# Sample attention scores: one float32 product per key block in place of three split ones

## The chip, the cores and the metric

The kernel runs on one core of a Trainium2 chip. The metric is the device time of one execution in microseconds (us). Engines are named as in the profile: PE is TensorE's matmul row and PEld its weight loads, DVE is VectorE, ACT is ScalarE, POOL is GpSimd, SP is the engine that issues most DMAs.

## The reference, cut to what matters

One layer of a hybrid decoder handles a prompt of 1024 tokens and eight samples of eight new tokens each. Every sample has 1024 cached positions, in pages that a table names. Two attention groups of six heads read them: stick-breaking attention and forgetting attention (FoX). For both, the scores of the new tokens against the cached keys are

```python
kb_all = jnp.concatenate([gather_pages(cache_sb_k[l], page_table), kb], axis=1)
b_out = stick_breaking(qb, kb_all, vb_all, q_pos, k_pos)
kc_all = jnp.concatenate([gather_pages(cache_fox_k[l], page_table), kc], axis=1)
c_out = forgetting_attention(qc, kc_all, vc_all, F[:, past:], F, q_pos, k_pos)
# in both: z = einsum('bthd,blhd->bhtl', q.astype(float32), k.astype(float32)) * HEAD_DIM ** -0.5
```

Everything is float32, and the change concerns only these products `z` over cached keys.

## The kernel before, in words

Nearly all matmuls of this kernel work on values that are split by hand: a float32 value x becomes a high part (x rounded to the type float32r) and a low part (x minus the high part, again float32r), and a product of two values is the sum of high by high, high by low and low by high: three matmuls into the same PSUM bank. ACT usually makes the high part by a copy that rounds, and DVE the low part by a subtraction.

The program runs in stages: the input projections; then the prompt's attention (`prompt_attention`) beside the last projections; then, from about 402 us, `sample_attention` beside the rest of the prompt's attention; then the rest of `sample_attention` beside `merge` (the output projection, tile `prod`); then, from about 846 us, the feed-forward network. Where two generators run side by side, `conduct` takes turns between them by weights written into their `yield`s; after that a scheduler arranges the instructions of each engine's queue. Each engine works through its queue in order.

`sample_attention` goes through 32 steps t (group FoX first, then stick-breaking; in each group four pairs of samples; in each pair two halves of the pages for each of the two samples). In a step:

- `k_load` fetches 512 cached key rows by an indirect DMA on POOL (tile `kr`, three buffers).
- `k_tr` runs three times (p = 0, 1, 2, a pair of heads each). PE transposes four blocks of 128x128 into a PSUM bank (tile `str`, L713). ACT rounds the bank into the high part of `kt` (L717), DVE subtracts to get the low part (L718).
- `qk` of the step before does the scores: for each p three matmuls of 512 columns (tile `sqk`, L748), with the queries' high or low part as the stationary operand. `queries` picks them out of `qz`, which `build_q` fills for each pair of samples (L674).
- After a pair's two halves the scores go to the softmax (FoX, DVE L756) or the sigmoids (stick-breaking, ACT L760 and L761). `a_tr` transposes the pair's weights (tile `satr`, L802) and splits them (tile `ats`, L804 and L805); `v_split` splits value rows (tile `vh`, L816 and L817), and `value` multiplies (tile `spv`, L829).

The prompt's attention uses `aqk` (scores), `atr` (transposes of the weights, split by ACT L576 and DVE L577) and `apv` (values).

PSUM's eight banks are two rings: three banks for the uses marked "a", five for those marked "b" (`NBANK`, `BANKS`). A use takes the next bank of its ring when the one that stood there has been read out. `sqk`, `satr`, `spv`, `apv` and `prod` are in the ring of three; `str`, `atr`, `aqk`, `spick`, `stat` and `spread` in the ring of five.

Of the kernel before, what the change touches and what calls it, by code (L numbers as in the profile page):

```python
# [10 lines left out]
F32 = mybir.dt.float32  # L11
F32R = mybir.dt.float32r
I32 = mybir.dt.int32
AF = mybir.ActivationFunctionType
OP = mybir.AluOpType
# [28 lines left out]
RING = {"at": 5, "at_s": 2, "at_g": 2, "vh": 4, "kt": 3, "kr": 3, "vr": 3, "sa_x": 3, "vo": 2, "zn": 2, "hl": 2,  # L44
        "k32": 2, "ko": 2, "vt": 1, "wraw": 2, "wsplit": 5, "pvt": 2, "sl": 2}
# [5 lines left out]


NBANK = {"a": 3, "b": 5}
BANKS = {"pqk": "a", "ptok": "a", "kout": "a", "apv": "a", "sqk": "a", "satr": "a", "spv": "a", "prod": "a",
         "fgu": "a", "fgs": "b", "spread": "b", "fgt": "b", "aqk": "b", "atr": "b", "str": "b", "spick": "b", "gate": "b",
         "stat": "b", "fout": "b"}

# [42 lines left out]
def tile_decode_step(ctx, tc, x_prompt, x_sample, cache_sb_k, cache_sb_v, cache_fox_k, cache_fox_v,  # L100
# [5 lines left out]
    V, A, G, T, S = nc.vector, nc.scalar, nc.gpsimd, nc.tensor, nc.sync  # L106

    def f(ap):
        return ap.bitcast(F32)

    def pool(stack, name, bufs=1, space=None, side=None):
        kw = {} if space is None else {"space": space}
        if space is not DRAM:
            kw["reuse_waits"] = "tile"
        return stack.enter_context(tc.tile_pool(name=name, bufs=bufs, side=side, **kw))
# [58 lines left out]
    kn, vn, qn = {}, {}, {}  # L174
# [8 lines left out]
    def bank(shape, use):  # L183
        return ps.tile(shape, F32, name=use, tag=BANKS[use], bufs=NBANK[BANKS[use]])

# [457 lines left out]
    def sample_attention(sa):  # L643

        cks_, cvs_ = (cache_sb_k, cache_fox_k), (cache_sb_v, cache_fox_v)
        sos, kts, scs, gts, ats, vhs, krs, vrs, pzs, pvs, mns, dts = ({} for _ in range(12))
        def where_k(t):

            return 1 - t // 16, t // 4 % 4, t % 2, t // 2 % 2
# [8 lines left out]
        c2 = sa.tile([128, C_END - C_NSB], F32, name="c2")  # L658
        S.dma_start(c2, consts[:, C_NSB:C_END])

        qz = sa.tile([128, 1216], F32R, name="qz")
        V.memset(f(qz), 0.0)
        zns = {}

        def build_q(u):

            g, sp = 1 - u // 4, u % 4
            qv = qz[:, 0:1200].rearrange("p (x c) -> p x c", c=400)
            for e in range(2):
                er = slice(e * 64, e * 64 + 64)  # L670
                for si in range(2):
                    src = f(qn[g][er, :, :, (2 * sp + si) * 8:(2 * sp + si) * 8 + 8])
                    o = si * 128 + e * 8
                    V.tensor_copy(qv[er, :, o:o + 200].rearrange("p x (a c) -> p x a c", c=8)[:, :, 0:25:24], src)  # L674

        def queries(p, a, si):
            o = p * 384 + a * 192 + si * 64
            return qz[:, o:o + 128]

        def new_scores(g):  # L680
# [27 lines left out]
        def k_tr(t, p):  # L708
            if p == 0:
                kts[t] = []  # L710
            pt = bank([128, 4, 128], "str")
            for j in range(4):
                T.transpose(pt[:, j, :], krs[t][:, j, p * 128:p * 128 + 128], ident)  # L713
            kt = sa.tile([128, 2, 512], F32R, name="kt", bufs=RING["kt"])
            kts[t].append(kt)
            ptf = pt.rearrange("p j k -> p (j k)")
            A.copy(kt[:, 0], ptf)  # L717
            V.tensor_tensor(kt[:, 1], ptf, f(kt[:, 0]), op=OP.subtract)  # L718

        def by_row(x):  # L720
            return x[:, 0:SP_].rearrange("q (p r) -> q r p", r=8)
# [18 lines left out]
        def qk(t):  # L740
            g, sp, si, hf = where_k(t)
            u = t // 4
            if si == 0:
                pzs[t // 2] = bank([128, 512], "sqk")
            pz = pzs[t // 2]
            for p in range(3):
                for n_, (a, b) in enumerate(((0, 0), (0, 1), (1, 0))):
                    T.matmul(pz, lhsT=queries(p, a, si), rhs=kts[t][p][:, b], start=si == 0 and p == 0 and n_ == 0,  # L748
                             stop=si == 1 and p == 2 and n_ == 2)
            del kts[t], krs[t]  # L750
            if si:
                pz = pzs.pop(t // 2).rearrange("q (r p) -> q r p", p=128)
                sc = by_row(scs[u])[:, hf * 4:hf * 4 + 4]
                if g:
                    mn = mns[u]
                    V.tensor_tensor_reduce(sc, pz, by_row(dts[u])[:, hf * 4:hf * 4 + 4], 1.0,  # L756
                                           mn[:, 0:1] if hf else 3.0e38, op0=OP.add, op1=OP.min,
                                           accum_out=mn[:, hf:hf + 1])
                else:
                    A.activation(sc, pz, AF.Sigmoid, scale=-1.0)  # L760
                    A.activation(by_row(gts[u])[:, hf * 4:hf * 4 + 4], pz, AF.Sigmoid)  # L761
# [99 lines left out]
        NT_ = 32  # L861
        mks = {}
        build_q(0)
        for t in range(NT_ + SVL + 2):
            tv = t - SVL
# [12 lines left out]
            if t < NT_:  # L878
                for p in range(2):
                    k_tr(t, p)  # L880
                    yield 0.43
            if 0 <= t - 1 < NT_:
                qk(t - 1)
                if t < NT_ and t % 4 == 0:
                    build_q(t // 4)
                yield 1.95
            if t < NT_:
                k_tr(t, 2)
                yield 0.43
# [327 lines left out]
    sa = pool(psa, "sa")  # L1217
    ppc = ExitStack()
    pcs.append(pool(ppc, "pc", side="right"))
    sam = sample_attention(sa)  # L1220
    conduct([(att, P_W3A[0]), (sam, P_W3A[1])], True)
    ppc.close()
# [395 lines left out]
    for f0, nf in [(0, 1)] + [(x, FCH) for x in range(1, NFF, FCH)]:  # L1618
# [8 lines left out]
        for i in (8, 0, 1, 2, 3, 4, 5, 6, 7):  # L1627
            o = slice(i * 128, i * 128 + 128)
# [42 lines left out]
```

## Time and profile before

| | us |
|---|---|
| median of 3 runs | 1602.29 (1601.11 to 1602.63) |
| the profiled execution's own time | 1605.99 |
| its span in the trace | 1604.1 |

The profiled execution took 3.7 us more than the median, and 1.9 us of it lie outside the span. The page gives the busy time of each engine, 40 slices of the span with the granted TensorE clock, the DMA queues, the chain of work that ended last, and groups of instructions. "idle before" in a group is time in which the engine had nothing to do just before these instructions, with the engine and line whose end released it.

### The profile page before, as it was taken

The page shows a single profiled execution, that of the slowest core. Times are in us where ns is not written, and L with a number is a line of the kernel's source. Part 1 is how long each engine was busy: PE and PEld are TensorE (multiplying, and loading weights), DVE is VectorE, ACT ScalarE, POOL GpSimd, SP SyncE. Part 2 cuts the span into 40 slices and gives each one's busy share as a digit, 9 for nine tenths or more (in the row PEclk, how much of TensorE's full clock was granted, in tenths as well). Part 3 has the DMA queues.
Part 4 walks back from the last instruction along what each step waited for, and adds up shares of the span by engine and source line. Part 5 has one row for each costly group of instructions (what it writes and reads, how often), then busy time and mean ns, then how long its engine had stood idle before and what let it go on. Part 6 is the DMA issues. An engine that isn't in the chain of part 4 may idle for free.

```text
span 1604.1 us, 26359 instructions
## 1 busy us (share of the span) xinstructions
PE 1509.9 (94%) x9580; PEld 1394.2 (87%) x9580; DVE 1033.4 (64%) x1887; ACT 703.9 (44%) x1472; POOL 679.9 (42%) x775
## 2 busy tenths in 40 slices
PE   7999999888799989988997999999999999999997
PEld 6999998888688878877887999999999997888886
DVE  5432368866698988988769565555555557555554
ACT  6424257455477788864434233333333323111113
POOL 1203375546535655565315544444454435111112
PEclk9999999999799999989998999999999999999999
DMA  6155565355869775675433122222222218322202
GB/s 179 50 168 172 192 198 162 92 156 164 263 181 264 218 207 167 212 266 160 129 144 87 55 71 75 74 71 82 75 75 81 82 60 330 109 82 81 82 1 112
DMA packets 148741, 217.60 MB, mean 136 GB/s; under 512 B 19156, under 2 KB 111684, under 8 KB 148612
## 3 DMA queue, kind: packets, MB, share of 16 engines
q1 hardware_dynamic: 138868, 163.72, 32.7%
q0 software_dynamic: 9744, 52.20, 9.9%
q8 instruction: 76, 1.25, 0.3%
q14 instruction: 53, 0.43, 0.1%
HBM read 163.95 MB, written 51.92 MB: 135 GB/s over the span
## 4 chain that ended last, share of the span: by engine, by line
PE 47%; DVE 4%; DMA 2%; POOL 1%; issue 1%; ACT 0%; SPq 0%; DVEq 0%; POOLq 0%; ACTq 0%
PE fout L1635 5%; PE fout L1634 5%; PE fgs L1362 5%; PE fgs L1360 5%; PE fgs L1361 5%; PE fout L1637 5%; PE fgu L1360 4%; PE fgu L1362 4%; PE fgu L1361 4%; PE prod L1152 1%; DMA lr<-linv 1%; PE prod L1153 1%; PE prod L1155 1%; PE fgu L1435 1%; PE fgu L1434 1%
## 5 line engine op out<-in xcount | busy, mean ns | idle before, releaser
L1634 PE MATMUL fout<-foh,g_h 128*128 128x512 f32 x378 | 148.1, 392 | 0.9 <-POOL g_h L1584 0.9
L1635 PE MATMUL fout<-fol,g_h 128*128 128x512 f32 x378 | 148.1, 392 | 0.6 <-DVE fol L1580 0.6
L1638 DVE TENSOR_TENSOR z<-fout,z 128x512 f32<-128x512 f32 x128 | 86.7, 688 | 95.1 <-PE fout L1637 95.0
L817 POOL TENSOR_TENSOR vh<-vr,vh 128x384 fp32r<-128x384 f32 x96 | 102.7, 1088 | 74.0 <-ACT vh L816 55.5
L1360 PE MATMUL fgu<-xh,ws 128*128 128x272 f32 x456 | 131.8, 289 | 0.0
L1360 PE MATMUL fgs<-th,ws 128*128 128x272 f32 x456 | 131.7, 289 | 0.0
L1362 PE MATMUL fgs<-th,ws 128*128 128x272 f32 x456 | 131.6, 289 | 0.0
L1362 PE MATMUL fgu<-xh,ws 128*128 128x272 f32 x456 | 131.5, 288 | 0.0
L1361 PE MATMUL fgu<-xl,ws 128*128 128x272 f32 x456 | 131.1, 287 | 0.0
L1361 PE MATMUL fgs<-tl,ws 128*128 128x272 f32 x456 | 131.0, 287 | 0.0
L1637 PE MATMUL fout<-foh,g_l 128*128 128x512 f32 x336 | 130.0, 390 | 0.4 <-POOL g_l L1585 0.4
L748 PE MATMUL sqk<-kt,qz 128*128 128x512 f32 x288 | 99.4, 438 | 3.2 <-ACT kt L717 1.3
L291 PE MATMUL pqk<-xh,wh 128*128 128x384 f32 (+1 forms) x288 | 96.9, 337 | 1.6 <-DVE pvt L604 1.0
L1347 DVE TENSOR_TENSOR ws<-s,ws 128x512 fp32r<-128x512 f32 x76 | 71.1, 935 | 42.4 <-ACT ws L1346 39.9
L292 PE MATMUL pqk<-xl,wh 128*128 128x384 f32 (+1 forms) x288 | 95.4, 332 | 0.0
L293 PE MATMUL pqk<-xh,wl 128*128 128x384 f32 (+1 forms) x288 | 94.5, 332 | 0.0
L1347 DVE TENSOR_TENSOR ws<-raw,ws 128x512 fp32r<-128x512 f32 x67 | 57.0, 854 | 54.0 <-ACT ws L1346 54.0
L1361 PEld LDWEIGHTS fgs<-tl,ws 128*128 128x128 f32 x456 | 86.0, 189 | 0.0
L1361 PEld LDWEIGHTS fgu<-xl,ws 128*128 128x128 f32 x456 | 86.0, 189 | 0.0
L1360 PEld LDWEIGHTS fgs<-th,ws 128*128 128x128 f32 x456 | 85.9, 188 | 0.0
L1360 PEld LDWEIGHTS fgu<-xh,ws 128*128 128x128 f32 x456 | 85.8, 188 | 0.0
L1583 ACT CAST g_h<-gr 128x1088 fp32r<-128x1088 f32 x21 | 23.1, 1101 | 142.8 <-PE fout L1635 137.4
(355 smaller groups left out, 4808.1 us busy)
## 6 DMA issues: line engine op xcount, KB each, us to landing
raw<-in_w_ffn_in_dram SPq DMA_DIRECT2D x43, 512.0 KB
gr<-gs SPq DMA_DIRECT2D x21, 544.0 KB
wor<-in_w_ffn_out_dram SPq DMA_DIRECT2D x21, 512.0 KB
qq<-qs SPq DMA_DIRECT2D x36, 256.0 KB
wraw<-in_w_in_dram SPq DMA_DIRECT2D x20, 384.0 KB
kk<-ks SPq DMA_DIRECT2D x24, 256.0 KB
vs<-vt SPq DMA_DIRECT2D x16, 384.0 KB
vv<-vs SPq DMA_DIRECT2D x12, 512.0 KB
```

Of the source, the lines that this page charges most:

```text
L291: T.matmul(pm[:, 0:n], lhsT=wh, rhs=xh[:, k, o], start=k == 0, stop=False)
L292: T.matmul(pm[:, 0:n], lhsT=wh, rhs=xl[:, k, o], start=False, stop=False)
L293: T.matmul(pm[:, 0:n], lhsT=wl, rhs=xh[:, k, o], start=False, stop=k == KT - 1)
L748: T.matmul(pz, lhsT=queries(p, a, si), rhs=kts[t][p][:, b], start=si == 0 and p == 0 and n_ == 0, stop=si == 1 and p == 2 and n_ == 2)
L817: (V if t >= 16 and j in VL else G).tensor_tensor(vh[:, 1], vrs[t][:, j], f(vh[:, 0]), op=OP.subtract)
L1347: V.tensor_tensor(x[:, 1], src, f(x[:, 0]), op=OP.subtract)
L1360: T.matmul(pm[:, 0:b - a], lhsT=w[:, 0, k], rhs=hi[:, k, a:b], start=k == 0, stop=False)
L1361: T.matmul(pm[:, 0:b - a], lhsT=w[:, 0, k], rhs=lo[:, k, a:b], start=False, stop=False)
L1362: T.matmul(pm[:, 0:b - a], lhsT=w[:, 1, k], rhs=hi[:, k, a:b], start=False, stop=k == 3)
L1634: T.matmul(pm, lhsT=gh[q][:, o], rhs=wh2[q][:, hs], start=q == 0, stop=False)
L1635: T.matmul(pm, lhsT=gh[q][:, o], rhs=wl2[q][:, hs], start=False, stop=i == 8 and end)
L1637: T.matmul(pm, lhsT=gl[q][:, o], rhs=wh2[q][:, hs], start=False, stop=end)
```

## The change

The keys and the queries of the cached scores are no longer split. `k_tr` copies the transposed block once, as float32: ACT for p = 0 and 2, DVE for p = 1. `build_q` adds the queries' high and low parts into one float32 tile. `qk` issues one matmul per p on float32 operands. `kt` has six buffers of half the size, in place of three. Besides this, `satr` moves from the ring of three PSUM banks to the ring of five.

```diff
-BANKS = {..., "satr": "a", ...
+BANKS = {..., "satr": "b", ...
...
-        qz = sa.tile([128, 1216], F32R, name="qz")
+        qz = sa.tile([128, 640], F32, name="qz")
...
-                    V.tensor_copy(qv[er, :, o:o + 200].rearrange("p x (a c) -> p x a c", c=8)[:, :, 0:25:24], src)
+                    V.tensor_tensor(qv[er, :, o:o + 8], hi, lo, op=OP.add)
...
-            kt = sa.tile([128, 2, 512], F32R, name="kt", bufs=RING["kt"])
+            kt = sa.tile([128, 512], F32, name="kt", bufs=6)
             kts[t].append(kt)
-            ptf = pt.rearrange("p j k -> p (j k)")
-            A.copy(kt[:, 0], ptf)
-            V.tensor_tensor(kt[:, 1], ptf, f(kt[:, 0]), op=OP.subtract)
+            (V.tensor_copy if p == 1 else A.copy)(kt, pt.rearrange("p j k -> p (j k)"))
...
             for p in range(3):
-                for n_, (a, b) in enumerate(((0, 0), (0, 1), (1, 0))):
-                    T.matmul(pz, lhsT=queries(p, a, si), rhs=kts[t][p][:, b], start=si == 0 and p == 0 and n_ == 0,
-                             stop=si == 1 and p == 2 and n_ == 2)
+                T.matmul(pz, lhsT=queries(p, si), rhs=kts[t][p], start=si == 0 and p == 0, stop=si == 1 and p == 2)
```

The queues are arranged anew from the first cached score on. Up to there PE's order is the same, and in the feed-forward network but for a few of its first matmuls. In the changed kernel `k_tr`'s transposes are L714, the copy L717, the score matmul L746, the weights' transposes L799.

On PE, where the FoX group's first pair of samples has its weights transposed (`satr`), these rows stand before:

```order
L802 MATMUL satr<-ct,sa_x 128x128 x4
L713 MATMUL str<-ct,kr 128x128 x4
L748 MATMUL sqk<-kt,qz 128x512 x3
L573 MATMUL atr<-ct,at_g 128x128
L713 MATMUL str<-ct,kr 128x128 x4
L526 MATMUL aqk<-kk,qq 128x512
L527 MATMUL aqk<-kf,qf 128x512
L748 MATMUL sqk<-kt,qz 128x512 x2
L802 MATMUL satr<-ct,sa_x 128x128 x4
L748 MATMUL sqk<-kt,qz 128x512
L713 MATMUL str<-ct,kr 128x128 x4
L802 MATMUL satr<-ct,sa_x 64x128
```

and these in the changed kernel:

```order
L746 MATMUL sqk<-kt,qz 128x512
L573 MATMUL atr<-ct,at_g 128x128 x3
L714 MATMUL str<-ct,kr 128x128 x4
L746 MATMUL sqk<-kt,qz 128x512
L526 MATMUL aqk<-kk,qq 128x384
L527 MATMUL aqk<-kf,qf 128x384
L587 MATMUL apv<-at,vv 128x256 x2
L526 MATMUL aqk<-kk,qq 128x384
L527 MATMUL aqk<-kf,qf 128x384
L799 MATMUL satr<-ct,sa_x 128x128 x8
L799 MATMUL satr<-ct,sa_x 64x128
L746 MATMUL sqk<-kt,qz 128x512
```

Three score matmuls have become one, and the pair's transposes of weights, which stood in three pieces between scores, stand together and some ten rows later against the prompt's work.

On DVE, at the same place in the program (the rows ISA are the FoX scores' reduction, L531 for the prompt and L756 or L753 for the samples), these rows stand before:

```order
L718 TENSOR_TENSOR kt<-str,kt 128x512
L531 ISA at_s,mn<-aqk,cz 128x128
L531 ISA mn 128x1
L531 ISA at_s,mn<-aqk,cz 128x256
L531 ISA mn 128x1
L718 TENSOR_TENSOR kt<-str,kt 128x512
L756 ISA sa_x,mns<-sqk,sa_x 128x4x128
L756 ISA mns 128x1
L531 ISA at_s,mn<-aqk,cz 128x384
L531 ISA mn 128x1
L805 TENSOR_TENSOR ats<-satr,ats 128x8x64
L718 TENSOR_TENSOR kt<-str,kt 128x512
```

and these in the changed kernel:

```order
L717 COPY kt<-str 128x512
L577 TENSOR_TENSOR at<-atr,at 128x4x128
L717 COPY kt<-str 128x512
L531 ISA at_s,mn<-aqk,cz 128x128
L531 ISA mn 128x1
L753 ISA sa_x,mns<-sqk,sa_x 128x4x128
L753 ISA mns 128x1
L531 ISA at_s,mn<-aqk,cz 128x256
L531 ISA mn 128x1
L531 ISA at_s,mn<-aqk,cz 128x384
L531 ISA mn 128x1
```

The subtractions that stood between the reductions of the scores are gone, and every third of them is a copy.

## Rows read from the trace of the kernel before

**Rows 1.** The page: busy time and share of the span; DVE in 40 slices, tenths.

```profile
PE 1509.9 (94%) x9580; PEld 1394.2 (87%) x9580; DVE 1033.4 (64%) x1887; ACT 703.9 (44%) x1472; POOL 679.9 (42%) x775
DVE  5432368866698988988769565555555557555554
```

**Rows 2.** Windows around sample attention: length, then busy time (instructions) of each engine.

```profile
core 0: us, PE busy (x) PEld busy (x) DVE busy (x) ACT busy (x) POOL busy (x), PEclk, DMA share, GB/s
402.00:440.00 38.00, 27.54 (x136) 23.17 (x135) 25.31 (x35) 17.46 (x36) 20.03 (x26) 0.77 0.85 260
440.00:560.00 120.00, 112.20 (x729) 100.55 (x729) 108.78 (x284) 87.25 (x194) 63.85 (x67) 0.97 0.77 220
560.00:715.00 155.00, 140.00 (x844) 122.31 (x844) 132.67 (x292) 124.42 (x249) 87.47 (x83) 0.94 0.69 222
715.00:846.00 131.00, 122.68 (x593) 101.05 (x592) 101.27 (x179) 58.09 (x122) 48.87 (x53) 0.98 0.44 142
```

**Rows 3.** Chain of work that ended last: start, length, piece.

```profile
707.14 0.67 DVE kt L718
...
713.82 0.59 PE stat L1091 x2
```

**Rows 4.** Groups of PE from 440 to 715 us: count, busy, mean ns, idle before.

```profile
L748 PE MATMUL sqk<-kt,qz 128*128 128x512 f32 x255 | 86.5, 433 | 2.3 <-DVE ats L805 1.1 <-DVE mns L756 0.8 <-ACT kt L717 0.3
L713 PE MATMUL str<-ct,kr 128*128 128x128 f32 x329 | 49.4, 277 | 1.8 <-DVE kt L718 1.4 <-DVE qz L674 0.2 <-DVE at L577 0.2
L829 PE MATMUL spv<-vh,ats 128*128 128x384 f32 x192 | 47.8, 364 | 3.1 <-DVE vh L817 1.7 <-ACT vh L816 0.5 <-DVE ats L805 0.5
L587 PE MATMUL apv<-at,vv 128*128 128x256 f32 x237 | 42.9, 298 | 4.2 <-ACT sa_x L761 2.5 <-issue 1.2 <-ACT kt L717 0.5
L573 PE MATMUL atr<-ct,at_g 128*128 128x128 f32 x231 | 37.2, 275 | 5.9 <-DVE sot L854 3.1 <-DVE mn L531 2.4 <-DVE kt L718 0.2
L526 PE MATMUL aqk<-kk,qq 128*128 128x384 f32 (+4 forms) x72 | 27.8, 387 | 1.7 <-DVE kt L718 0.7 <-DVE mn L531 0.6 <-DVE at L577 0.2
L527 PE MATMUL aqk<-kf,qf 80*128 80x384 f32 (+4 forms) x72 | 26.2, 364 | 0.0
L802 PE MATMUL satr<-ct,sa_x 128*128 128x128 f32 (+1 forms) x63 | 10.4, 279 | 0.5 <-DVE y L1158 0.4
L829 PE MATMUL spv<-vn,ats 128*128 128x384 f32 x24 | 6.9, 371 | 0.0
L847 PE MATMUL spick<-ct,vo 128*128 128x128 f32 x36 | 6.4, 289 | 0.0
L1152 PE MATMUL prod<-woh,ch 128*128 128x512 f32 x10 | 4.0, 401 | 0.0
...
L1091 PE MATMUL stat<-ct,sq 128*128 128x1 f32 x18 | 2.6, 254 | 3.4 <-POOL sq L1131 1.7 <-POOL sq L1129 1.7
```

**Rows 5.** Windows of PE alone, in the output product (512 columns) and the gate product (272).

```profile
1400.00:1440.00 40.00, 40.00 (x178) 1.00 0.24 82
1000.00:1040.00 40.00, 40.00 (x321) 1.00 0.24 76
```

**Rows 6.** Timeline of PE: four transposes in a row (start, length).

```profile
610.81 0.60 PE L573 MATMUL atr<-ct,at_g 128*128 128x128 f32 x4
```

**Rows 7.** Groups of the key blocks' split, whole span.

```profile
L717 ACT CAST kt<-str 128x512 fp32r<-128x512 f32 x96 | 55.4, 588 | 40.6 <-PE str L713 37.1 <-PE sqk L748 2.9
L718 DVE TENSOR_TENSOR kt<-str,kt 128x512 fp32r<-128x512 f32 x96 | 64.7, 680 | 12.6 <-ACT kt L717 12.0
```

**Rows 8.** One line, L985: a float32 copy out of PSUM on DVE (min/median/max ns).

```profile
L985 DVE COPY wt<-gate x1: 692/692/692, 49.1 to 49.1; 128x512 f32<-128x512 f32 x1
```

**Rows 9.** Timeline: two float32 matmuls of 48 columns, issued once each.

```profile
290.83 0.32 PE L404 MATMUL fgt<-lf,ct 128*128 128x48 f32 x2
290.99 0.39 PE L406 MATMUL fgt<-lf,ct 128*128 128x48 f32 x2
```

**Rows 10.** One line, L404: the two records' lengths (min/median/max ns).

```profile
L404 PE MATMUL fgt<-lf,ct x2: 203/238/273, 290.8 to 290.9; 128*128 128x48 f32 x2
```

More of the change, by code (lines that the diff above doesn't have):

```diff
@@ L53 @@
 NBANK = {"a": 3, "b": 5}
-BANKS = {"pqk": "a", "ptok": "a", "kout": "a", "apv": "a", "sqk": "a", "satr": "a", "spv": "a", "prod": "a",
+BANKS = {"pqk": "a", "ptok": "a", "kout": "a", "apv": "a", "sqk": "a", "satr": "b", "spv": "a", "prod": "a",
          "fgu": "a", "fgs": "b", "spread": "b", "fgt": "b", "aqk": "b", "atr": "b", "str": "b", "spick": "b", "gate": "b",
@@ L659, in sample_attention @@
         S.dma_start(c2, consts[:, C_NSB:C_END])
-        qz = sa.tile([128, 1216], F32R, name="qz")
-        V.memset(f(qz), 0.0)
+        qz = sa.tile([128, 640], F32, name="qz")
+        V.memset(qz, 0.0)
         zns = {}
@@ L667, in build_q @@
             g, sp = 1 - u // 4, u % 4
-            qv = qz[:, 0:1200].rearrange("p (x c) -> p x c", c=400)
+            qv = qz[:, 0:624].rearrange("p (x c) -> p x c", c=208)
             for e in range(2):
@@ L671, in build_q, with queries @@
                 for si in range(2):
-                    src = f(qn[g][er, :, :, (2 * sp + si) * 8:(2 * sp + si) * 8 + 8])
+                    hi, lo = (f(qn[g][er, :, a, (2 * sp + si) * 8:(2 * sp + si) * 8 + 8]) for a in range(2))
                     o = si * 128 + e * 8
-                    V.tensor_copy(qv[er, :, o:o + 200].rearrange("p x (a c) -> p x a c", c=8)[:, :, 0:25:24], src)
-        def queries(p, a, si):
-            o = p * 384 + a * 192 + si * 64
+                    V.tensor_tensor(qv[er, :, o:o + 8], hi, lo, op=OP.add)
+        def queries(p, si):
+            o = p * 192 + si * 64
             return qz[:, o:o + 128]
```

## The prediction

> **What bounds the kernel now.** The page first: PE is busy for 94% of the span, DVE for 64%, but DVE's slices run at 8 and 9 tenths from the eleventh to about the nineteenth, which is where sample attention lies [rows 1]. Outside these slices PE sets the pace, and there the change edits nothing. So the question is what this one stage is worth. The windows cut it up [rows 2]: a start from 402 to 440 us, in which the DMA engines are busy for 0.85 of the time and no engine is full; 440 to 715 us with all score matmuls that are left; and 715 to 846 us, the output projection, which has none. From 440 to 715 us DVE is busy for 108.8 + 132.7 = 241.5 of 275 us (88%), ACT for 211.7 (77%).
>
> PE's 252.2 busy us there say too much, since a matmul's record includes its way through the array. Two windows show what PE needs when nothing holds it: 178 matmuls of 512 columns in 40 us, 225 ns each, and 321 of 272 columns, 125 ns each [rows 5]; between them a column costs 0.42 ns and a matmul 11 ns, so 384 columns take 171 ns and 256 take 118. Four transposes in a row last 0.60 us; without the last one's own 0.275 us (the group's mean, [rows 4]) three steps are 0.325, so one takes 0.11 us [rows 6]. By the counts of [rows 4]: 255 score matmuls 57.4 us; 329 + 231 + 63 + 36 transposes 72.5; 192 + 24 `spv` 36.9; 237 `apv` 28.0; 144 `aqk` (256 to 512 columns, some 0.18 us) 25.9; 3 x 10 `prod` 6.8; 18 `stat` at a transpose's price 2.0. That is 229.5 of 275 us, 83%. PE loses 45.5 us there, in many short waits. Of the 22.9 us that the groups show as idle before a matmul, DVE ended 13.5 (59%), ACT 3.8 (17%), POOL 3.4, and 1.2 nothing that is shown [rows 4]. So DVE is the fullest engine and the one that PE waits for most, and PE is not far behind. The chain that ended last can be followed back to about 703 us only; a subtraction of `kt` is one of its pieces, and from there it goes through the output projection to the end [rows 3]. What the stage saves should therefore arrive at the end in full.
>
> **The change part by part.** *DVE.* 96 subtractions go, 64.7 us [rows 7]; 32 copies of a 128x512 PSUM bank come. The one such float32 copy on DVE took 692 ns [rows 8], so 22.1 us. DVE gives back 42.6 us of work, and the 12.0 us that it idled for the rounding copy of `kt` on ACT [rows 7] has no successor of its kind. From 440 to 715 us it has 85 of the 96 (255 / 3): its load falls by 85 x 0.680 - 28 x 0.692 = 38 us, from 88% to 74%.
>
> *ACT.* 32 of 96 copies of 588 ns go, 18.8 us [rows 7]. That the rest write float32 in place of float32r I count at nothing: at the same size on the same engine the worst that I can argue is the 692 ns of DVE, 64 x 0.1 = 6.7 us on an engine with 63 us of slack.
>
> *PE.* 288 matmuls of 512 columns go, 288 x 0.225 = 64.8 us. In their place stand 96 float32 products, which the trace doesn't show at this width. It shows small ones. A float32 matmul that the code issues once is two records (L404 and L406, x2 each) [rows 9]. If each record streamed its columns once, the product would cost 2 x 225 = 450 ns and all 96 would cost 43.2 us: 21.6 us less than before. That is the lower bound. L404's two records last 0.32 us together and the last one 0.273 [rows 9, 10], so the second began 0.047 us after the first, for 48 columns: 0.98 ns a column (0.88 to 1.08 with the rounding), twice the 0.42 of the split matmuls and a little more. At 0.98 ns a record of 512 columns takes 0.50 us and all 192 take 96 us: 31 us more than before, the upper bound. I take two streams per record, four per product, 4 x 0.225 = 0.90 us, since the small records' excess over twice 0.42 is of the size of a matmul's fixed part: 96 x 0.90 = 86.4 us, 21.6 us more than before.
>
> The Trainium skill, FP8 and Floating Point Precision, section TensorE Precision Notes, says that true FP32 takes four passes through the array, one for each product of a high or low half with the other's. By that rule PE pays the 21.6 us; by the count of records alone it would be given them.
>
> *Waits.* A score matmul waited for a copy on ACT and then a subtraction in DVE's full queue; now it waits for one copy. Behind it in PE's queue stand the prompt's scores and transposes and the samples' values, so a late copy holds them as before. The copies for p = 1 sit in DVE's queue behind the prompt's reductions. `kt` has six buffers in the same bytes, so transposes are not held by it.
>
> *The ring.* `satr` takes 24 banks of the ring of five in place of the ring of three. PE's waits that a freer ring of three could end are those for `ats`, 1.1 + 0.5 us [rows 4]. On the other side a bank of `satr` stays taken for the two reads of a split, 0.588 + 0.680 us if priced as `kt`'s [rows 7]; if `str`, `atr` and `aqk` waited for all 24 in full, that would be 30 us. The order shows each pair's transposes in one piece among PE work that doesn't need their banks, so I count nothing.
>
> *The rest.* 32 small additions replace 32 small copies that fill `qz`; the DMAs stay the same in number and size.
>
> **The sum.** PE's need in the stage rises by 21.6 us. Against this stands the part of its lost 45.5 us that ends. I take DVE's 59% in full, since DVE gets 14 points of slack, and half of ACT's 17%, since ACT gets 6: 0.67 x 45.5 = 30.6 us. The stage gains 9.0 us: 1606.0 - 9.0 = 1597.0 on the scale of the profiled execution. The median lies 3.7 us lower, so 1593.3.
>
> **The rivals.** *PE becomes the bound and keeps its losses (slower).* After the change PE needs 229.5 + 19.1 = 249 of 275 us, 90% of the stage as it now lasts. If its short waits are the time from one engine's end to the next one's start and not DVE's backlog, they stay, and the stage grows by 21.6 us, or by 21.6 / 0.83 = 26 if they grow with it: 1624 to 1628. For it: half of the 45.5 us shows as no idle time at all, and every product is now a block of 0.9 us behind which short transposes wait. Against it: DVE idles for only 33.5 of these 275 us. It decides below 21.6 us recovered; a recovery between 0 and 18 gives 1606 to 1624.
>
> *A wash.* 18 to 25 us recovered: within 3.2 us of the time before. About 0.2% is what a measurement of this kernel can tell from no change.
>
> *More than forecast.* PE packs as tightly as its queue allows: all 45.5 us recovered would give -24. The granted clock of 0.97 and 0.94 [rows 2] means some 7 and 19 us at 1.2 in place of 2.4 GHz; a PE that pauses less may keep the higher level there, up to 13 us that are part of the 45.5. Recoveries of 36 to 45 give 1578 to 1588. Against it: the DMA engines are already busy for 0.77 and 0.69 of these windows.
>
> *A record streams once.* PE gets 21.6 us back, and with 30.6 us of waits the stage would gain up to 52 us, less what ACT, DVE and the page loads then hold: 1550 to 1570. L404's second record speaks against it.
>
> **How the numbers follow.** Forecast (26 to 36 us recovered, 1588 to 1599) 0.40; more 0.17; record streams once 0.04; wash 0.14; slower 0.25. Faster by over 0.2% is then 0.61, within it 0.14, slower 0.25. The time is the forecast's, 1593. The range leaves out the single-stream case, the slowest half of the slower case and the best of the better one, some 0.18 in all: 1576 to 1614.
>
> **What would show it.** 192 records of `sqk` matmuls from `kt` about 0.45 us apart and not 0.22; `kt` on DVE 32 times at 0.69 us and on ACT 64 times at 0.59; DVE's load in the stage at some 75%; PE's waits for DVE smaller than 13.5 us; the first `fgu` matmul of the feed-forward network some 9 us earlier. I am wrong if records stream once, or if PE, denser in need, still loses more than 27 us between 440 us and the stage's end.

## The result

The changed kernel takes 1613.56 us (median of 4 runs, 1611.85 to 1614.13), the kernel before 1601.7 beside it (4 runs, 1599.74 to 1602.63). The ratio is 1.0058, with a 95% interval of 1.0039 to 1.0078: slower by 0.6%, some 9.3 us, where 9.0 us less were forecast. The two medians lie further apart, 11.9 us or 0.74%; against the medians of the kernel before that stand beside the experiments (1603.58 to 1604.18 us, 20 to 29 runs each) 1613.56 is 0.58 to 0.62% more, which is what the ratio says. The profiled execution took 1614.13 us, its span is 1612.4.

**The profile after.** First the page and the windows, for [rows 1, 2].

```profile
PE 1516.8 (94%) x9484; PEld 1374.4 (85%) x9484; DVE 1007.7 (62%) x1823; ACT 685.6 (43%) x1440; POOL 668.0 (41%) x775
DVE  5433368866578857788769765555555558555554
```

```profile
402.00:440.00 38.00, 31.12 (x149) 22.45 (x149) 19.63 (x31) 18.37 (x37) 23.86 (x29) 0.84 0.89 279
440.00:560.00 120.00, 113.99 (x672) 90.55 (x673) 98.13 (x258) 78.03 (x179) 62.75 (x65) 0.99 0.76 221
560.00:715.00 155.00, 140.18 (x780) 110.93 (x779) 113.11 (x257) 113.08 (x229) 80.41 (x81) 0.93 0.67 213
715.00:846.00 131.00, 123.02 (x592) 102.51 (x590) 98.04 (x175) 57.15 (x119) 49.94 (x52) 0.96 0.43 142
```

DVE did get its slack: 98.1 + 113.1 = 211.2 of 275 us, 77% and no longer 88%. What the key blocks cost now is in the view of the tile `kt` (count, shortest, median and longest ns, first and last start), for [rows 7], and in one piece of PE's timeline:

```profile
L746 PE MATMUL sqk<-kt,qz x192: 590/592/1061, 407.8 to 717.3; 128*128 128x512 f32 x192
L717 ACT COPY kt<-str x64: 561/585/632, 403.6 to 713.0; 128x512 f32<-128x512 f32 x64
L717 DVE COPY kt<-str x32: 661/682/692, 406.6 to 706.7; 128x512 f32<-128x512 f32 x32
```

```profile
409.69 1.88 PE L746 MATMUL sqk<-kt,qz 128*128 128x512 f32 x4
```

Four records last 1.88 us and the last one 0.592, so they start (1.88 - 0.592) / 3 = 0.429 us apart, and a product of two records costs PE 0.858 us. The same view of the kernel before has the last score matmul at 708.3 us:

```profile
L748 PE MATMUL sqk<-kt,qz x288: 388/397/776, 406.3 to 708.3; 128*128 128x512 f32 x144
```

So the last one starts 9.0 us later, and the span is 8.3 us longer. 96 products cost 96 x (0.858 - 0.675) = 17.6 us more than three split matmuls each; about 17.6 - 9.0 = 8.6 us of PE's losses were given back, not 30.6. PE's groups from 440 to 715 us, for [rows 4], show which waits are left:

```profile
L746 PE MATMUL sqk<-kt,qz 128*128 128x512 f32 x161 | 82.2, 605 | 0.0
L826 PE MATMUL spv<-vh,ats 128*128 128x384 f32 x192 | 53.8, 387 | 7.8 <-DVE vh L814 5.1 <-POOL vh L814 1.9 <-ACT vh L813 0.7
L714 PE MATMUL str<-ct,kr 128*128 128x128 f32 x324 | 48.7, 280 | 1.2 <-DVE sot L851 1.2
L587 PE MATMUL apv<-at,vv 128*128 128x256 f32 x231 | 44.2, 309 | 2.7 <-DVE mns L753 2.7
L573 PE MATMUL atr<-ct,at_g 128*128 128x128 f32 x224 | 35.9, 278 | 8.0 <-DVE ats L802 7.1 <-DVE mn L531 0.8
L526 PE MATMUL aqk<-kk,qq 128*128 128x384 f32 (+4 forms) x72 | 33.1, 459 | 2.2 <-DVE kt L717 0.9 <-DVE at L577 0.8 <-DVE mn L531 0.6
```

With DVE less busy, PE waited longer for it: 5.1 + 1.2 + 2.7 + 7.1 + 0.8 + 0.9 + 0.8 + 0.6 = 19.2 us, before 13.5. ACT's part fell from 3.8 to 0.7 us and POOL's from 3.4 to 1.9; all idle time before matmuls is 21.9 us, before 22.9. So by this estimate most of the 8.6 us that were given back had not shown as idle time.

**Why DVE was late though it had time.** DVE's own waits from 402 to 720 us (what waited, for what: us in total, times, longest), in the kernel before and then in the changed one:

```profile
DVE sa_x L736 <- DMA sa_x<-fsn: 13.0, 3, 7.2
DVE kt L718 <- ACT kt L717: 12.0, 15, 1.4
DVE zn L773 <- DMA za<-zs: 4.7, 1, 4.7
DVE at L577 <- ACT at L576: 4.0, 5, 2.6
```

```profile
DVE at L577 <- ACT at L576: 13.9, 17, 2.0
DVE sa_x L735 <- DMA sa_x<-fsn: 12.3, 2, 8.4
DVE zn L770 <- DMA za<-zs: 9.5, 1, 9.5
```

The 12.0 us for ACT's rounding copy of `kt` are gone, but the wait for ACT's half of the prompt's split (`at`) grew from 4.0 to 13.9 us. The largest of PE's waits for DVE in the changed kernel, 7.1 us before an `atr`, can be followed in the timeline (start, length, idle before and its releaser):

```profile
584.33 1.22 ACT L801 CAST ats<-satr 128x512 fp32r<-128x512 f32 x3
585.06 0.67 DVE L802 TENSOR_TENSOR ats<-satr,ats 128x512 fp32r<-128x512 f32 x1
595.22 0.36 DVE L770 TENSOR_TENSOR zn<-za,c 128x64 f32<-128x64 f32 x2 [9.48 <-DMA za<-zs]
595.49 0.87 DVE L802 TENSOR_TENSOR ats<-satr,ats 128x512 fp32r<-128x512 f32 x2
596.24 0.48 PE L573 MATMUL atr<-ct,at_g 128*128 128x128 f32 x1 [7.07 <-DVE ats L802]
```

From 585.7 to 595.2 us DVE did nothing. The next instruction in its queue was a 0.2 us sum of the new tokens' scores (`zn`), which waited for data on the way to DRAM and back; the subtraction of `ats`, for which PE's queue stood still, was behind it, though ACT had done its half by 585.6 us. "Waited for DVE" here meant "for a DMA in front of DVE". In the kernel before the same sum starts at nearly the same time:

```profile
594.74 0.36 DVE L773 TENSOR_TENSOR zn<-za,c 128x64 f32<-128x64 f32 x2 [4.71 <-DMA za<-zs]
```

DVE came to it 4.3 us later there, since it had more to do, and stood for 4.71 us in place of 9.48. Less work on DVE did not bring the data sooner; it only made DVE stand longer. The Trainium skill, TensorE: Matmul & The Clock Gate, section Architectural detail: the array is 16× 32×32, not 1× 128×128, says that DVE's queue is strict FIFO; the trace agrees, with 9.48 us idle before `zn` and the `ats` subtraction 0.27 us after its start. The chain that ended last, which breaks off at about 703 us in the kernel before [rows 3], goes back through the whole stage here, and its six longest pieces in it are all DMAs (start, length):

```profile
399.83 19.41 DMA sa_x<-fsn
430.85 8.07 DMA sa_x<-fsn
504.51 4.65 DMA sa_x<-fsp
543.90 7.40 DMA kf<-ks
577.37 5.87 DMA zs<-zt
583.97 11.15 DMA za<-zs
```

The first three feed the subtraction L735 of `dt`, the forget gates that `begin` fetches at a pair's start. The first two stand before 440 us, in a window that the prediction named and then left. `kf` belongs to the prompt's scores; no experiment below touches it.

### The profile page after: what moved, and what is told of

It reads as the page before. It is cut to its first block, busy times and chain, and to the rows that moved or that the text cites. A ratio compares the mean times of both kernels' runs of the same rounds, so it can differ in the third digit from the quotient of the medians.

```text
span 1612.4 us, 25995 instructions
## 1 busy us (share of the span) xinstructions
PE 1516.8 (94%) x9484; PEld 1374.4 (85%) x9484; DVE 1007.7 (62%) x1823; ACT 685.6 (43%) x1440; POOL 668.0 (41%) x775
## 4 chain that ended last, share of the span: by engine, by line
PE 77%; DVE 8%; DMA 8%; ACT 3%; issue 2%; POOL 1%; SPq 1%; DVEq 0%; POOLq 0%; ACTq 0%
PE fout L1632 5%; PE fout L1631 5%; PE fgs L1359 5%; PE fgs L1357 5%; PE fout L1634 5%; PE fgs L1358 5%; PE fgu L1357 4%; PE fgu L1359 4%; PE fgu L1358 4%; PE sqk L746 4%; PE pqk L291 3%; PE pqk L293 3%; PE pqk L292 3%; PE apv L587 2%; PE spv L826 2%
## 5 line engine op out<-in xcount | busy, mean ns | idle before, releaser
L746 PE MATMUL sqk<-kt,qz 128*128 128x512 f32 x192 | 98.5, 608 | 0.0
L577 DVE TENSOR_TENSOR at<-atr,at 128x512 fp32r<-128x512 f32 (+2 forms) x144 | 76.6, 545 | 22.9 <-ACT at L576 21.3
L1632 PEld LDWEIGHTS fout<-fol,g_h 128*128 128x128 f32 x378 | 71.5, 189 | 18.2 <-DVE fol L1577 3.2
```

The lines of the kernel that those rows point to most:

```text
L746: T.matmul(pz, lhsT=queries(p, si), rhs=kts[t][p], start=si == 0 and p == 0, stop=si == 1 and p == 2)
L1632: T.matmul(pm, lhsT=gh[q][:, o], rhs=wl2[q][:, hs], start=False, stop=i == 8 and end)
```

## The experiments

Ratios are to the kernel before, with their 95% intervals; 1% is 16.0 us.

### The ring alone

`satr` back to the ring of three in the changed kernel (the diff), and to the ring of five in the kernel before:

```diff
-BANKS = {..., "satr": "b", ...
+BANKS = {..., "satr": "a", ...
```

> The changed kernel with the weights' transposes (satr) back in the ring of three banks; all else as changed. Theory A (PE's longer products, 17.6 us more need by the 429 ns between records, are paid almost in full, and DVE's relief is worth only some 8 us): 1610 to 1617 us, as the changed kernel. Theory B (the move of satr, with the order that follows from it, costs the time: in the trace of the changed kernel PE waits 7.1 us for one reading of satr's bank): 1602 us or less.

> The kernel before with satr moved to the ring of five and nothing else. Theory A: within 3 us of the kernel before, 1599 to 1605. Theory B: slower by about the whole change, 1609 to 1615.

1.0075 (1.0057 to 1.0092) and 0.9998 (0.9983 to 1.0013). In the kernel before the move is worth nothing that can be measured; in the changed one its taking back costs at most a little, 0.17% against 1.0058 with overlapping intervals. PE's wait of 7.1 us above was one for a bank: `atr` takes its banks from the ring of five, where `satr` now stood. With the ring back this wait is gone and the time is no better; PE's longest wait from 440 to 715 us is then one of 5.3 us for ACT (L576).

### The price on PE

The changed kernel's copies, with n float32r matmuls of the rounded operands in place of the float32 product, so that the low parts are left out (the diff has n = 3):

```diff
-                T.matmul(pz, lhsT=queries(p, si), rhs=kts[t][p], start=si == 0 and p == 0, stop=si == 1 and p == 2)
+                for n_ in range(3):
+                    T.matmul(pz, lhsT=queries(p, si), rhs=kts[t][p], start=si == 0 and p == 0 and n_ == 0,
+                             stop=si == 1 and p == 2 and n_ == 2)
```

> The changed kernel with each float32 product replaced by three float32r matmuls of the same two operands, so that PE's load is that of the kernel before while DVE and ACT keep their relief (the keys' and queries' low parts are left out: three times the product of the rounded values). Theory A: PE's 17.6 us come back nearly whole, 1595 to 1600, faster than the kernel before by what the relief is worth. Theory B: at least 1606, since ring and order stay.

> The changed kernel with each float32 product replaced by one float32r matmul (the low parts are left out), so that PE's need is 43 us under the kernel before and 61 us under the changed one. If PE's need sets the pace of this stage: the three short ones measured 0.9971 of before, and 0.8 of 43 us less is 1560 to 1570 us. If the stage is held by other things once PE has room (the loads, ACT, the samples' chain from scores to values): 1582 to 1595.

> The changed kernel with each float32 product replaced by four float32r matmuls of the same operands (low parts left out): PE's need is 86 us in place of the 82 us of the float32 products, but in four short pieces instead of two records of 429 ns. If the need alone counts: 1612 to 1620, as the changed kernel or a little more. If the length of a block counts, behind which short transposes wait: 1598 to 1607.

And a fourth matmul, low by low, in the kernel before:

```diff
-                for n_, (a, b) in enumerate(((0, 0), (0, 1), (1, 0))):
+                for n_, (a, b) in enumerate(((0, 0), (0, 1), (1, 0), (1, 1))):
```

> The kernel before with a fourth float32r matmul per key block, low by low: PE's need grows by 21.6 us and no other engine's does. If PE's need is paid by some 0.8 here as between the three short ones and the change: 1618 to 1625. If DVE, at 88% of the stage, is the bound that hides PE's work in the kernel before: 1602 to 1609.

| kernel | PE's need against before (estimate, us) | ratio |
|---|---|---|
| three short | 0 | 0.9971 (0.9954 to 0.9987) |
| changed | +17.6 | 1.0058 (1.0039 to 1.0078) |
| four short | +21.6 | 1.0066 (1.0043 to 1.0089) |
| one short | -43.2 | 0.9877 (0.9851 to 0.9902) |
| before, four products | +21.6 | 1.0096 (1.007 to 1.0122) |

Three short is the experiment that matters: DVE and ACT have the changed kernel's relief, PE its old need.

```profile
L747 PE MATMUL sqk<-kt,qz x288: 388/396/775, 406.1 to 697.8; 128*128 128x512 f32 x144
```

It gains 0.29%, 4.6 us. That is all that the relief was worth at PE's old need, where the prediction had 30.6. From there to the changed kernel it is 1.0058 - 0.9971 = 0.87%, 13.9 us, for 17.6 us of PE's work. Not all of that has to be PE's work: the queues are arranged anew, and from 402 to 720 us DVE stands for 7.3 + 5.5 + 1.0 = 13.8 us at `dt` and `zn` in three short, and for 12.3 + 9.5 = 21.8 us in the changed kernel. The kernel before with four products is the cleaner case, with 7.8 + 6.4 + 3.9 = 18.1 us of such stands against 13.0 + 4.7 = 17.7. Four matmuls of a quarter of the product's length cost about what the float32 product does: by this it is the need that counts, not the longer block that short transposes stand behind. Work that is added to PE costs 0.7 to 0.8 of itself (13.9 of 17.6; 15.2 of 21.6; in the kernel before 15.4 of 21.6); work that is taken away gives back 0.35 (15.1 of 43.2). So PE's need sets the stage's length when it grows, and only in part when it shrinks.

### DVE's load

All 96 copies on ACT, once with 96 subtractions on DVE whose result nobody reads (the last two lines of the diff), once without them:

```diff
-            (V.tensor_copy if p == 1 else A.copy)(kt, pt.rearrange("p j k -> p (j k)"))
+            A.copy(kt, pt.rearrange("p j k -> p (j k)"))
+            kx = sa.tile([128, 512], F32, name="kx", bufs=1)
+            V.tensor_tensor(kx, pt.rearrange("p j k -> p (j k)"), kt, op=OP.subtract)
```

> The changed kernel with all copies on ACT and a DVE subtraction of 512 columns per key block kept, whose result nobody reads, so that DVE and ACT are loaded as before and PE as changed. Theory A: the relief's 8 us are lost on top, 1618 to 1625. Theory C (DVE's relief is worth nothing in this stage, PE's waits being latency): 1611 to 1616, as the changed kernel.

> The changed kernel with all 96 copies on ACT: DVE loses 22 us more, ACT has its load of before. If relief of DVE is worth little: 1610 to 1617, as the changed kernel. If DVE's queue still delays the key copies: 1604 to 1609.

1.0082 (1.0062 to 1.0103) with them, 1.0022 (1.0005 to 1.004) without. 96 x 0.685 = 65.8 us of DVE's work, more than the change took away, are worth 0.6%, 9.6 us. This need not be load alone: the subtraction also reads the bank of `str` after ACT and so gives it back later. And ACT alone is 0.36% better than a third of the copies on DVE, though this makes ACT the fuller engine (204.5 us against DVE's 192.8 from 440 to 715 us).

### DVE's place in its queue

Two edits let DVE reach these instructions later, when their data are there. The sum `zn` is tied to the pair's own scores, `za` gets a second buffer and `new_scores` is called at step 14 and not 18 (three things at once, not tried one by one); the subtraction of `dt` is tied to a column `kl` of a key block of the pair's second step (`begin_late`, called in the third):

```diff
-            if t in (0, 18):
+            if t in (0, 14):
...
-            zn = zns[g] = sa.tile([128, 4, NS], F32, name="za", bufs=1)
+            zn = zns[g] = sa.tile([128, 4, NS], F32, name="za", bufs=2)
...
-                V.tensor_tensor(zn, z, c2[:, sp * 64:sp * 64 + 64], op=OP.add)
+                one = small.tile([128, 1], F32, name="one", bufs=4)
+                V.tensor_scalar(one, scs[u][:, 4:5], 0.0, 1.0, op0=OP.mult, op1=OP.add)
+                V.scalar_tensor_tensor(zn, z, one, c2[:, sp * 64:sp * 64 + 64], op0=OP.mult, op1=OP.add)
...
-            V.tensor_scalar(dt[:, 0:NTOK], dt[:, 0:NTOK], fq[:, sp:sp + 1], None, op0=OP.subtract)
+        def begin_late(u, t):
...
+            dt, kl = dts[u], kts[t][2]
...
+            V.scalar_tensor_tensor(fl, kl, 0.0, fq[:, sp:sp + 1], op0=OP.mult, op1=OP.add)
+            V.tensor_scalar(dt[:, 0:NTOK], dt[:, 0:NTOK], fl, None, op0=OP.subtract)
```

The `zn` edit alone, in the changed kernel and in the kernel before:

> The changed kernel, with the stick-breaking group's new-token scores made four steps earlier and the DVE instruction that adds their mask (zn) tied to the pair's cached scores, so that DVE does not stand in its queue for the DMA that brings them (9.5 us in the changed kernel's trace, 4.7 us before). If such standing is a large part of what PE loses in the changed kernel: 1602 to 1608 us. If it is made up for later in the stage anyway: 1610 to 1616.

> The same edit in the kernel before. If the 4.7 us of standing are paid there: 1597 to 1601, and the distance to the changed kernel with this edit is what the long products cost, 5 to 9 us. If not paid: 1601 to 1606.

Both edits, with all copies on ACT and in the kernel before:

> The changed kernel with all copies on ACT, the edit of the new-token scores, and the FoX group's forget terms (dt) tied in the same way to a key block, so that DVE does not stand for their DMA either (12.3 us in the changed kernel's trace). If DVE's standing is what PE waits for: 1592 to 1600, the best of the float32 versions. If PE's need sets the pace: 1604 to 1609, as with all copies on ACT alone.

> The kernel before with both edits (13.0 and 4.7 us of standing). If standing counts: 1590 to 1598, faster than both kernels. If not: 1600 to 1606.

Both with the changed kernel's copies, and each by itself:

> The changed kernel with both stands of DVE taken away (the new tokens' sum asked for later, the subtraction of dt tied to a later kt), the copies of p = 1 left on DVE. If the stands for DMAs account for what the all-on-ACT kernel with both edits gained over the one without them (1.0022 to 0.993), the copies' place matters little once DVE doesn't stand: 0.993 to 0.997 of before. If the copies must leave DVE as well, since they sit there behind the prompt's reductions, 0.999 to 1.003 (1.0058 less a part). At 1.004 or more, neither stand mattered here.

> All 96 copies on ACT (1.0022 alone), and of the two edits only the later subtraction of dt, which waited for fsn's DMA. If this is the stand that counts, 0.992 to 0.996 of before. If it is the other one, za's, 1.000 to 1.003. If each gives a half, 0.997 to 0.999.

> All 96 copies on ACT (1.0022 alone), and of the two edits only the later sum zn with a second buffer of za. If za's stand is the one that counts, 0.992 to 0.996 of before. If it is dt's, 1.000 to 1.003, or worse, as the same edit made the kernel before 0.5% slower. If each gives a half, 0.997 to 0.999.

> The kernel before with the later subtraction of dt alone. The sum edit alone gave 1.0048 here and both gave 1.0008; if they add, dt's alone gives 0.996, and then the fair partner of the float32 kernel at its best is this one, and float32 is worth some 0.3%. If before is held by DVE's load and not by its stands, 0.999 to 1.001, and float32 scores are worth some 0.7% once DVE's queue is cleared.

| edits | before | changed | changed, all copies on ACT |
|---|---|---|---|
| none | 1 | 1.0058 (1.0039 to 1.0078) | 1.0022 (1.0005 to 1.004) |
| `zn` | 1.0048 (1.003 to 1.0066) | 1.0031 (1.0014 to 1.0047) | 0.9975 (0.9958 to 0.9992) |
| `dt` | 0.9971 (0.9956 to 0.9986) | not run | 0.9954 (0.9937 to 0.9971) |
| both | 1.0008 (0.9991 to 1.0025) | 0.9987 (0.9969 to 1.0005) | 0.993 (0.9907 to 0.9953) |

In the changed kernel the two edits are worth 1.0058 - 0.9987 = 0.71%, 11 us, and with the copies on ACT 0.92%, 15 us; there `zn` alone gives 0.47% and `dt` alone 0.68%. In the kernel before they are worth nothing together: `dt` gains 0.29%, `zn` costs 0.48%. With `zn` alone there, DVE's 4.7 us for `za` are gone, but it stands for 18.9 us for ACT's half of `kt`, before 12.0, and for 15.5 us for `fsn`, before 13.0. With everything the float32 kernel takes 1594.04 us (the kernel before 1603.84 beside it); its windows and its last score matmul:

```profile
402.00:440.00 38.00, 35.21 (x185) 25.92 (x183) 23.66 (x39) 24.77 (x49) 24.35 (x28) 0.92 1.00 285
440.00:560.00 120.00, 115.81 (x694) 92.15 (x693) 93.37 (x256) 85.95 (x200) 64.29 (x67) 1.00 0.80 232
560.00:715.00 155.00, 141.31 (x787) 110.02 (x785) 115.42 (x246) 125.45 (x247) 90.07 (x88) 0.99 0.67 213
```

```profile
L755 PE MATMUL sqk<-kt,qz x192: 590/592/1057, 405.8 to 697.9; 128*128 128x512 f32 x192
```

The last score matmul starts 19.4 us earlier than in the changed kernel (697.9 against 717.3), though DVE is as busy from 440 to 715 us (208.8 us against 211.2). Its longest waits there are

```profile
DVE at L577 <- ACT at L576: 19.6, 21, 3.9
DVE qz L674 <- PE sqk L755: 8.1, 5, 3.9
```

and neither `fsn` nor `za` is among them. The kernel before with both edits has lost its stands for `za` and most of those for `fsn` as well, but DVE is still full there (110.5 + 130.7 = 241.2 of 275 us), and it waits for ACT's half of the split (waits, then windows):

```profile
DVE kt L718 <- ACT kt L717: 16.3, 13, 4.4
DVE sa_x L745 <- DMA sa_x<-fsn: 2.9, 1, 2.9
```

```profile
440.00:560.00 120.00, 110.39 (x716) 98.90 (x715) 110.46 (x286) 85.20 (x194) 63.39 (x65) 0.97 0.81 226
560.00:715.00 155.00, 136.99 (x829) 118.91 (x828) 130.69 (x287) 128.91 (x252) 86.33 (x83) 0.97 0.67 215
```

Copies of p = 1 on DVE cost 0.36%, 0.56% and 0.57% in the three rows where the last two columns can be compared. With both edits and these copies DVE's queue stands for PE at them, as it did for the DMAs, for 10.7 us where the changed kernel has 5.4:

```profile
DVE kt L717 <- PE str L714: 10.7, 8, 4.5
```

The expectations that one stand would account for all, or that the copies' place would matter little, were wrong. The `zn` edit alone missed both of its ranges in both kernels: 1609.65 us in the changed kernel lies between them, 1612.48 in the kernel before above them. Against the best form of the kernel before, the one with the `dt` edit, the best float32 form is 0.9971 - 0.993 = 0.4% faster, and the two intervals just miss each other (0.9956 and 0.9953); with the `dt` edit alone in both, 0.9954 against 0.9971, no difference is shown.

## Why the prediction was wrong, point by point

- **Four passes: right, the term a little too large.** The records are 0.429 us apart, not 0.45, so the term of 21.6 us is 17.6. The Trainium skill, FP8 and Floating Point Precision, section TensorE Precision Notes, counts four passes for true FP32; the trace agrees: 4 x 512 columns in 858 ns are 0.42 ns a column, the price of a float32r column. The end in which a record streams once is out.
- **The copies: right.** ACT's take 0.585 us, DVE's 0.682, for 0.588 and 0.692; DVE's load is 77%, for 74 to 75%.
- **The ring at nothing: right in the time.** The ring alone gives 0.9998 in the kernel before. It did bring PE its one long wait for a bank, of 7.1 us.
- **What the stage loses arrives at the end: right.** Last score matmul +9.0 us, span +8.3.
- **The step that failed: "I take DVE's 59% in full, since DVE gets 14 points of slack, and half of ACT's 17%", 0.67 x 45.5 = 30.6 us.** The changed kernel recovered some 8.6 us; with PE's old need the relief is worth 4.6 (three short). Two things went wrong in it. First, 0.67 was applied to 45.5 us, of which only 22.9 show as idle; no row gave the other 22.6 to DVE or ACT. DVE's 13.5 and half of ACT's 3.8 alone are 15.4 us, less than the 17.6 that PE got: with them the same sum gives a slower kernel. Second, the share of 59% was read off idle time that DVE *ended*, and taken for time that DVE's *load* caused. Load it was only in part: all of the subtractions and more are worth 9.6 us (load back). Another part was the order in DVE's queue behind two instructions that wait for DMAs, and taking instructions out leaves that in place; the view of DVE's own waits showed 13.0 and 4.7 us of it before the change (7.2 of the 13.0 before 440 us, outside the window of the 59%), beside the 12.0 us for ACT that the prediction did read [rows 7]. Those 12.0 us went, as it said, but the wait for ACT's half of `at` grew by 9.9.
- **The forecast sum with measured terms.** The relief -4.6, PE's need +13.9: +9.3 us, which is the result. These two are one path from before to after, so the sum has to close; what it shows is the size of each, the second with the stands that differ.
- **The rivals.** It went the way of "PE becomes the bound and keeps its losses", in the part with a recovery between 0 and 18 us. Its reason, that the short waits are the time from one engine's end to the next one's start, holds only in part: once DVE doesn't stand for the DMAs and has no copies to wait for, the float32 kernel is 1.3% faster than as changed (1.0058 to 0.993).
- **The tests set down.** PE's waits for DVE grew to 19.2 us in place of falling below 13.5. With 8.6 of 45.5 us given back PE still lost some 37, above the 27 that the prediction had named as the sign of being wrong (estimate). The first `fgu` matmul starts at 838.5 us and not 834.6: 3.9 us later, not 9 earlier.

Shown is that the kernel with the relief and PE's old need gains 4.6 us, that PE's work costs most of itself when it is added, that the two edits and the move to ACT give the time back, and that the stands go from the trace with them. Only argued is how much of it is DVE's wait itself: every edit rearranges all queues, and no run holds the order fixed. The `zn` edit, which costs the kernel before 0.48%, shows that differences of that size can come with an edit that was meant to help. Open is why ACT's half and `fsn` come later to DVE there, and what the `dt` edit does in the changed kernel with copies on DVE.

## What to carry to other kernels

"Idle, ended by engine X" is not X's load. Before crediting a lighter X, read X's own waits: an engine that works in order and stands at its queue's head for a DMA makes everyone behind it late, and less work on it doesn't bring that instruction's data sooner. And when work goes to the engine that is nearest to its bound, count most of its need (here 0.7 to 0.8 of it), and measure the relief elsewhere by an experiment with the need held fixed.

## What the runs showed of the hardware

- A float32 matmul of 512 columns is issued once and recorded as two, 429 ns apart: 858 ns a product, 3.8 times the 225 ns of a float32r matmul.
- A small transfer can land late while much else is moved: `fsn`, 12 KB an issue, took 19.41 us on the chain while the DMA engines were busy for 0.89 of the window from 402 to 440 us. It was issued behind `fsp` of 192 KB, so how much of this is its own isn't shown.
- Where PE stood for DVE, the granted clock fell. The stretch before, the one that holds most of the wait of 7.1 us and what follows it, and then the second stretch in the kernel before, where DVE's stand left PE no such wait:

```profile
560.00:592.00 32.00, 29.17 (x183) 24.03 (x181) 19.11 (x55) 22.98 (x44) 13.48 (x15) 1.00 0.83 234
592.00:606.00 14.00, 8.69 (x34) 7.43 (x35) 8.91 (x25) 9.02 (x21) 5.31 (x5) 0.51 0.15 33
```

```profile
592.00:606.00 14.00, 10.89 (x57) 9.49 (x58) 11.13 (x26) 8.91 (x21) 10.14 (x7) 0.76 0.22 57
```

From 592 to 606 us the mean is 0.51 in the changed kernel, so nearly all of it was at 1.2 of 2.4 GHz, though PE was at work again from 596.2 us. So the wait cost more than its 7.1 us; how much more no run shows by itself. In the float32 kernel without the stands the clock from 560 to 715 us is 0.99, and 0.93 as changed.
